# Turning three heads' normed outputs through memory with the DMA crossbar instead of on TensorE

## The chip, the cores and the metric

The kernel runs on one core of one Trainium2 chip. The metric is the device time of one execution in microseconds (us). The core has a matrix engine (TensorE, PE in the profile, with PEld for its weight loads), VectorE (DVE), ScalarE (ACT), GpSimd (POOL) and SyncE (SP), and 16 DMA engines. SyncE, ScalarE and GpSimd can issue DMAs. Each engine works through its own instructions in order.

## The reference, cut to what matters

The program is a two-layer generator trunk over 256 latent and 256 context tokens, 512 rows in all. Layer 0 uses an mLSTM mixer with four heads, layer 1 latent attention, and each is followed by a gated ConvFFN. The change sits in the mixer of layer 0, at its end:

```python
def out(h_in, s):
    Bq, T, _ = h_in.shape
    o = jax.nn.sigmoid(h_in @ w_og).reshape(Bq, T, M_HEADS, M_DV)
    hsum = o * s.transpose(0, 2, 1, 3).astype(h_in.dtype)
    return _head_rms_norm(hsum, norm_g) @ w_out
```

Each head has 512 columns (M_DV). Its gated output is divided by its root mean square over these columns, scaled with norm_g column by column, and the four heads side by side (2048 columns) are multiplied by w_out. Everything is in float32.

## The kernel before

Float32 products are made of three passes in a reduced-precision float32 (F32R): each operand is held as a high and a low part, and mm3 (line 427) issues high x high (L430), high x low (L433) and low x high (L434). The instructions are written in program order and a planner orders them on each engine: it takes, of what it expects to be ready, what comes first in the program. Tiles of one tag share a fixed number of buffers ("s2" has 15 buffers of 128x512 float32, "u" has 31 of 128x1024, "w" three), and an instruction that needs a buffer waits until one of its tag is free.

The weights come in one fixed order (class Stream): SyncE loads a block of 128x1024 (L308) into "raw", ScalarE casts it into the high part (L345), VectorE subtracts for the low part (L368), and TensorE reads both.

Background work is written as generators in k.bg. tick() advances the first generator in the list by one step after each chunk of the foreground product, so a generator starts only when the ones before it have ended; drain() runs all to the end.

The order in build() around the change:

- For each head h of four, w_qk (L999) makes its queries and keys: eight chunks of 24 matmuls of 512 columns, two ticks after each. Beside it run post(h-2), which norms and turns the output of the head two before, and head(h-1) (L1041), which makes that head's attention-like matrix and transposes it on TensorE into "PT" (L1118). Late in it v_load (L1128) loads v and the gate o ("oh") from memory into s2 buffers.
- av (L1163) multiplies PT with v, and VectorE multiplies the gate into the result (L1178): four tiles tt of 128 rows x 512 columns, in the buffers of "oh". s_mm makes the scores of the next head.
- After the last head the output product begins. outmm (L1524) runs over k = 0 to 15 (128 columns of the 2048 each, four per head) into "y" for the 256 context rows; a step k is twelve matmuls of 512 columns. k = 0 to 7 (heads 0 and 1) run with head(3) and post(2) beside them, and v_steps loads v and the gate of head 3. Then av(3); then k = 8 to 11 (head 2) with post(3) beside; then k = 12 to 15 (head 3). After that the same sixteen k for the 256 latent rows, from the same hn.

post (L1183) takes the four tiles tt of one head. ScalarE squares them and sums the rows (L1188), one Sqrt, VectorE the reciprocal (L1190) and the product with it (L1192). Then for each of four column groups e, TensorE transposes the four 128x128 blocks (L1198) into one PSUM tile "hnT", ScalarE writes it times norm_g as the high part (L1205) and VectorE the low part (L1206) of hn[k], k = 4h + e. hn[k] holds 128 columns on the partitions and all 512 rows along the free axis.

Of the kernel before, what the change touches and what calls it, by code (L numbers as in the profile page):

```python
# [7 lines left out]
F32 = mybir.dt.float32  # L8
F32R = mybir.dt.float32r
I32 = mybir.dt.int32  # L10
AF = mybir.ActivationFunctionType
ALU = mybir.AluOpType
AX = mybir.AxisListType
# [20 lines left out]
NB, NRAW, NU, NS = 3, 3, 31, 15  # L34
# [366 lines left out]
class K:  # L401
# [41 lines left out]
    def split(self, hi, lo, src):  # L443
        self.nc.scalar.copy(hi, src)
        self.nc.vector.tensor_sub(lo, src, hi)

    def smc(self, name):
        o, n = self.off[name]
        return self.sm0[:, o:o + n] if o < NSM0 else self.sm[:, o - NSM0:o - NSM0 + n]
# [25 lines left out]
    def setup(self):  # L475
# [3 lines left out]
        self.sm0 = p.tile([128, NSM0], F32, name="sm0")  # L479
        jp = p.tile([128, 128], I32, tag="s2", name="jp", bufs=NS)  # L480
        nc.gpsimd.iota(jp, pattern=[[1, 128]], base=0, channel_multiplier=-1)
# [88 lines left out]
    def ada_all(self, items):  # L570
# [14 lines left out]
        for r in self.bc:  # L585
            nc.scalar.activation(r, r, AF.Silu)  # L586
        yield
# [5 lines left out]
    def mod_tile(self, k):  # L593
# [3 lines left out]
        for g in range(2):  # L597
# [4 lines left out]
            else:  # L602
                nc.scalar.activation(v, v, AF.Identity, bias=sh[:, k, c:c + 1], scale=sc[:, k, c:c + 1])

    def start_up(self):
# [41 lines left out]

        self.tc.keep_in_program_order(nc.scalar.activation(self.tiny(1, "pre"), self.keps, AF.Silu))
        e = mybir.EngineType
# [3 lines left out]
        with self.tc.manual_schedule(engines={e.PE, e.DVE, e.Activation}):  # L653
            for _ in range(WARM):
                nc.tensor.matmul(idle, self.zero[:, 0:128], self.zero, start=True, stop=True)
            for step in STEPS:
                op, n = step[0], [int(x) for x in step[1:]]
                g = n[0]
                if op == "Q":
                    nc.scalar.activation(self.cond[:, :, 0:2], self.smc("cond").rearrange("p (a b) -> p a b", b=2),  # L660
                                         AF.Silu)
                    nc.vector.tensor_scalar(self.ident, self.jp, 0.0, None, op0=ALU.is_equal)
# [24 lines left out]
                elif op == "e":  # L687
# [3 lines left out]
                    nc.vector.tensor_scalar(x[:, c], x[:, c], sc[:, 1:2], sh[:, 1:2], op0=ALU.mult, op1=ALU.add)  # L691
                    nc.scalar.activation(h[:, 0, l], x[:, l], AF.Identity, bias=sh[:, 0:1], scale=sc[:, 0:1])
                    nc.vector.tensor_copy(h[:, 0, c], x[:, c])
# [31 lines left out]
    def conv(self, ps, w3, b, tmp, n):  # L725
        nc = self.nc
        nseg = n // 256
        nc.scalar.activation(tmp[:, :n], ps[:, :n], AF.Identity, bias=b, scale=w3[1])
        t3 = tmp[:, :n].rearrange("p (s t) -> p s t", s=nseg)
# [450 lines left out]
        self.PT = self.vh = self.oh = None  # L1180
        return r

    def post(self, h, tt):  # L1183
        nc = self.nc
        ss = self.tiny(4, "ss")
        jk = self.s2("jk")
        for t in range(4):
            nc.scalar.activation(jk, tt[t], AF.Square, accum_out=ss[:, t:t + 1])  # L1188
        nc.scalar.activation(ss, ss, AF.Sqrt, bias=self.keps, scale=1.0 / 512.0)
        nc.vector.reciprocal(ss, ss)  # L1190
        for t in range(4):
            nc.vector.tensor_scalar(tt[t], tt[t], ss[:, t:t + 1], None, op0=ALU.mult)  # L1192
        yield
        g = self.smc("mng")
        for e in range(4):
            pt = self.ps("hnT")
            for t in (2, 0, 1, 3):
                q = nc.tensor.transpose(pt[:, t * 128:(t + 1) * 128], tt[t][:, e * 128:(e + 1) * 128], self.ident)  # L1198
                if e or t != 2:
                    self.behind(q, [lead])  # L1200
                else:
                    lead = q
            k = h * 4 + e
            u = self.u("hn")
            nc.scalar.activation(u[:, 0], pt, AF.Copy, scale=g[:, k:k + 1])  # L1205
            nc.vector.scalar_tensor_tensor(u[:, 1], pt, g[:, k:k + 1], u[:, 0], op0=ALU.mult, op1=ALU.subtract)  # L1206
            self.hn[k] = u
        yield


    def bcast(self, row, name):
# [123 lines left out]
    def aout_fin(self, o1, pl, xr, gate, fi, h1u, att):  # L1335
# [86 lines left out]
        def cols(t, pts, n):  # L1422
            mod(t, 0, pts)
            for k in range(0, n, 2):
                mod(t, k + 1, pts)
                split(t, k, 0)
                split(t, k + 1, 0)
                if k + 2 < n:
                    mod(t, k + 2, pts)
                split(t, k, 1)  # L1430
                split(t, k + 1, 1)
# [750 lines left out]
def build(tc, off, a, out):  # L2182
    es = ExitStack()
    with es:
        k = K(tc, es, off, a)
        nc = k.nc
# [12 lines left out]
        k.bg2.append(k.ada_all([(0, 3, 4, 8)] + [(l, c, 0, 8) for l, c in ((0, 4), (0, 5), (1, 0), (1, 1), (1, 2), (1, 3), (1, 4), (1, 5))]))  # L2199
        S = None  # L2200
        tt = None
        k.hn = {}
        for h in range(H0):
            gens = []
            if h == 0:
                gens.append(k.gate_chain())
            if h >= 2:
                gens.append(k.post(h - 2, tt))
            if h >= 1:
                gens.append(k.head(h - 1, S))  # L2210
            k.bg = gens
            k.w_qk(h, 2, (lambda: k.v_load(h - 1)) if h >= 1 else None)
            k.drain()
            if h >= 1:
                tt = k.av(h - 1)
            S = k.s_mm(h)
        k.xc = None
        hn = lambda i: (k.hn[i][:, 0], k.hn[i][:, 1])
        pc = k.acc4()
        k.bg = [k.head(3, S, True), k.post(2, tt)]  # L2220
        vs = k.v_steps(3)
        for i in range(8):
            k.outmm("mout", range(i, i + 1), hn, pc, 0, 16, 2, n2=ADA_M)
            next(vs, None)
        k.drain()
        tt = k.av(3)
        k.bg = [k.post(3, tt)]
        k.outmm("mout", range(8, 12), hn, pc, 0, 16, 1, n2=ADA_M)
        k.drain()
        tokr = a["tok"].rearrange("(t p) d -> t p d", p=128)  # L2230
# [19 lines left out]
        pl = k.acc4()  # L2250
# [70 lines left out]
        pl = k.acc4(True)  # L2321
# [18 lines left out]
        pl = k.acc4(True)  # L2340
# [22 lines left out]
```

## Time and profile before

| | us |
|---|---|
| time, median of 3 runs | 1346.94 |
| lowest and highest of them | 1346.42 and 1347.75 |
| span of the profiled execution | 1345.3 |
| TensorE busy in that span | 1334.9 |
| VectorE busy | 1059.0 |
| ScalarE busy | 711.7 |
| GpSimd busy | 141.5 |

The times are of whole executions; the span is from the first to the last instruction of one profiled execution. A row of the profile names the line of the kernel, the engine, the operation, and output <- inputs by the program's names. "waits" rows say who waited for whom: total us, times, longest. A timeline row begins with its start and its length in us. An issue row gives the number of DMAs, KB each, and the median us from issue to landing.

### The profile page before, as it was taken

Reading aid. Unit: us, or ns where it says so; the run is one execution under the profiler, and the core shown is the slowest. Engines: PE = TensorE matmul, PEld = TensorE weight load, DVE = VectorE, ACT = ScalarE, POOL = GpSimd, SP = SyncE. Lnnn points to the kernel's source line nnn. Section 1 sums busy time; section 2 is a strip of 40 time slices with the busy share of each in tenths; the row PEclk is TensorE's granted clock in tenths of the full one; section 3 lists DMA queues with packets and bytes.
Section 4 is the critical chain, followed back from the end, with each engine's and each line's share of the span. In section 5 each row is a group of like instructions: output and inputs, shape, how many; then the busy total and the mean of one; then the engine's idle time right before and its main releaser. Section 6 shows DMA issues by size and latency. Waiting matters only on the chain.

```text
span 1345.3 us, 18750 instructions
## 1 busy us (share of the span) xinstructions
PE 1334.9 (99%) x6659; PEld 1120.2 (83%) x6659; DVE 1059.0 (79%) x1745; ACT 711.7 (53%) x1252; POOL 141.5 (11%) x236
## 2 busy tenths in 40 slices
PE   9999999999999999999999999999999999999997
PEld 5777888888888888888898888888888998988886
DVE  4798656678688696897979977758899889898874
ACT  4765444445744546474644334333566767676660
POOL 0222000011101011020002011111000002000100
PEclk9999999999999999999999999999999999999999
DMA  9988848889686384776628989967866437376750
GB/s 364 330 277 279 281 163 248 233 272 307 235 281 230 102 255 149 228 292 222 215 86 261 328 260 286 282 181 184 300 223 194 157 104 219 127 212 189 263 189 32
DMA packets 99885, 304.02 MB, mean 226 GB/s; under 512 B 12312, under 2 KB 25112, under 8 KB 99712
## 3 DMA queue, kind: packets, MB, share of 16 engines
q1 hardware_dynamic: 62992, 218.65, 48.6%
q0 software_dynamic: 26000, 66.75, 17.9%
q10 hardware_dynamic: 10800, 17.44, 3.6%
q8 instruction: 52, 0.85, 0.3%
q14 instruction: 41, 0.34, 0.1%
HBM read 272.21 MB, written 42.12 MB: 234 GB/s over the span
## 4 chain that ended last, share of the span: by engine, by line
PE 97%; DMA 1%; DVE 1%; ACT 0%; issue 0%; SPq 0%; DVEq 0%; ACTq 0%
PE fin L1503 8%; PE tok L430 6%; PE tok L434 6%; PE tok L433 6%; PE fin L433 6%; PE fin L434 6%; PE y L433 6%; PE fin L430 6%; PE y L434 6%; PE y L430 6%; PE qk L430 4%; PE qk L433 4%; PE qk L434 4%; PE up L718 2%; PE up L430 2%; PE up L434 1%
## 5 line engine op out<-in xcount | busy, mean ns | idle before, releaser
L368 DVE TENSOR_TENSOR w<-raw,w 128x1024 fp32r<-128x1024 f32 (+2 forms) x286 | 343.2, 1203 | 131.9 <-ACT w L345 129.7
L345 ACT CAST w<-raw 128x1024 fp32r<-128x1024 f32 (+2 forms) x286 | 296.2, 1037 | 282.4 <-PE tok L434 77.8
L544 DVE SCALAR_TENSOR_TENSOR junk<-ar,bc 128x1024 f32<-128x1024 f32 x128 | 156.1, 1219 | 5.2 <-ACT bc L586 2.3
L433 PE MATMUL fin<-h,w 128*128 128x512 f32 (+1 forms) x370 | 139.6, 377 | 0.0
L430 PE MATMUL fin<-h,w 128*128 128x512 f32 (+1 forms) x370 | 139.5, 377 | 0.0
L434 PE MATMUL fin<-h,w 128*128 128x512 f32 (+1 forms) x370 | 139.3, 377 | 0.0
L1503 PE MATMUL fin<-h,w 128*128 128x512 f32 (+1 forms) x636 | 111.1, 337 | 0.0
L1503 PEld LDWEIGHTS fin<-h,w 128*128 128x128 f32 x636 | 97.6, 190 | 13.2
L430 PE MATMUL qk<-xc,w 128*128 128x512 f32 x256 | 100.2, 391 | 0.0
L434 PE MATMUL qk<-xc,w 128*128 128x512 f32 x256 | 99.8, 390 | 0.0
L433 PE MATMUL qk<-xc,w 128*128 128x512 f32 x256 | 99.6, 389 | 0.0
L433 PEld LDWEIGHTS fin<-h,w 128*128 128x128 f32 x370 | 69.6, 188 | 13.0
L430 PEld LDWEIGHTS fin<-h,w 128*128 128x128 f32 x370 | 69.6, 188 | 12.9
L434 PEld LDWEIGHTS fin<-h,w 128*128 128x128 f32 x370 | 69.6, 188 | 12.6
L434 PEld LDWEIGHTS qk<-xc,w 128*128 128x128 f32 x256 | 48.0, 188 | 10.1
L430 PEld LDWEIGHTS qk<-xc,w 128*128 128x128 f32 x256 | 48.1, 188 | 9.8
L433 PEld LDWEIGHTS qk<-xc,w 128*128 128x128 f32 x256 | 48.1, 188 | 9.8
L430 PE MATMUL tok<-w,hT 128*128 128x512 f32 x128 | 49.9, 390 | 0.0
L433 PE MATMUL tok<-w,hT 128*128 128x512 f32 x128 | 49.8, 389 | 0.0
L434 PE MATMUL tok<-w,hT 128*128 128x512 f32 x128 | 49.8, 389 | 0.0
L735 ACT ACTIVATE fg<-fg 128x512 f32<-128x512 f32 (+1 forms) x44 | 23.1, 525 | 50.0 <-DVE fg L733 43.9
L368 DVE TENSOR_TENSOR wu<-raw,wu 128x1024 fp32r<-128x1024 f32 (+1 forms) x37 | 43.8, 1203 | 3.5 <-ACT wu L345 3.2
(486 smaller groups left out, 3125.7 us busy)
## 6 DMA issues: line engine op xcount, KB each, us to landing
raw<-in_ws SPq DMA_DIRECT2D x282, 512.0 KB, 4.5
ar<-in_adaT SPq DMA_DIRECT2D x80, 512.0 KB, 6.0
t4d<-in_ws POOLq DMA_DIRECT2D x20, 512.0 KB, 9.1
adaw<-in_ada SPq DMA_DIRECT2D x16, 512.0 KB, 8.0
zr<-fd ACTq DMA_DIRECT2D x33, 128.0 KB, 4.6
xmd<-xr POOLq DMA_DIRECT2D x16, 256.0 KB, 4.4
xcd<-cv POOLq DMA_DIRECT2D x16, 256.0 KB, 4.9
xs<-xmd POOLq DMA_DIRECT2D x16, 256.0 KB, 6.0
```

The lines of the kernel that those rows point to most:

```text
L345: self.cast = k.nc.scalar.copy(h[:, :cols], src)
L368: i = self.k.nc.vector.tensor_sub(l[:, :n], src, h[:, :n])
L430: q = mm(out, w[0], x[0], start=start, stop=False, skip_group_check=on)
L433: mm(out, w[0], x[1], start=False, stop=False, skip_group_check=on)
L434: mm(out, w[1], x[0], start=False, stop=stop, skip_group_check=on)
L544: nc.vector.scalar_tensor_tensor(o, w, 1.0, self.bc[j], op0=ALU.mult, op1=ALU.mult, accum_out=col[:, k, j:j + 1])
L718: nc.tensor.matmul(ps[m], wk[i][:, c], hT[k][:, j], start=made[m] == 0, stop=made[m] == 23)
L735: nc.scalar.activation(tmp[:, :n], tmp[:, :n], AF.Silu)
L1503: self.nc.tensor.matmul(ps[:, 0:256] if x else ps, w[x][:, k * 128:(k + 1) * 128], h[:, 0:256] if x else h, start=i == 0 and not k0, stop= ...
```

## The change

For heads 0, 1 and 2, post ends after the norm. ScalarE writes each normed tile as two planes of 16-bit halves (first the even half words of a row, then the odd ones), GpSimd writes the planes to memory, and the head and its place in memory are put in a list. A new generator turn_heads, placed behind head() in k.bg, takes it from there: SyncE issues four crossbar-transposing DMAs, one for each column group, each reading 1024 rows of 128 half words (two per token, one of each plane) and leaving 128 partitions of 1024 half words, which are the 512 float32 words in their order. From these SBUF tiles "hx" ScalarE and VectorE make the high and low part of hn as before. Head 3 (last=True) is turned on TensorE as before.

```diff
+U16 = mybir.dt.uint16
...
+    def planes(self, dst, src):
+
+        i = self.nc.scalar.copy(dst, src.bitcast(U16).rearrange("p (n h) -> p h n", h=2))
+        return i
...
-    def post(self, h, tt):
+    def post(self, h, tt, last=False):
...
         for t in range(4):
             nc.vector.tensor_scalar(tt[t], tt[t], ss[:, t:t + 1], None, op0=ALU.mult)
         yield
+        if not last:
+            d = self.dr.tile([512, 2, 512], U16, name="hd")
+            for t in range(4):
+                pl = self.pool.tile([128, 2, 512], U16, tag="s2", name="pl", bufs=NS)
+                self.planes(pl, tt[t])
+                nc.gpsimd.dma_start(d[t * 128:(t + 1) * 128], pl)
+            self.turned.append((h, d))
+            yield
+            return
         g = self.smc("mng")
...
+    def turn_heads(self):
+
+        nc, g = self.nc, self.smc("mng")
+        h, d = self.turned.pop(0)
+        v = d.rearrange("t h n -> (t h) n")
+        xs = []
+        for e in range(4):
+            x = self.s2("hx")
+            nc.sync.dma_start_transpose(x.bitcast(U16), v[:, e * 128:(e + 1) * 128])
+            xs.append(x)
+            if e % 2:
+                yield
+        for e in range(4):
+            k, x = h * 4 + e, xs[e]
+            u = self.u("hn")
+            nc.scalar.activation(u[:, 0], x, AF.Copy, scale=g[:, k:k + 1])
+            nc.vector.scalar_tensor_tensor(u[:, 1], x, g[:, k:k + 1], u[:, 0], op0=ALU.mult, op1=ALU.subtract)
+            self.hn[k] = u
+            xs[e] = x = None
+            if e % 2:
+                yield
...
-        k.hn = {}
+        k.hn, k.turned = {}, []
...
             if h >= 1:
                 gens.append(k.head(h - 1, S))
+            if h >= 2:
+                gens.append(k.turn_heads())
...
-        k.bg = [k.head(3, S, True), k.post(2, tt)]
+        k.bg = [k.head(3, S, True), k.post(2, tt), k.turn_heads()]
...
-        k.bg = [k.post(3, tt)]
+        k.bg = [k.post(3, tt, True)]
```

## The prediction

> **What bounds the kernel now.** I read the span and clock of the core first, then the page's busy shares and the chain that ended last, then all waits of TensorE.
>
> ```profile
> core 0: 1345.3 us, clock 0.998
> PE 1334.9 (99%) x6659; PEld 1120.2 (83%) x6659; DVE 1059.0 (79%) x1745; ACT 711.7 (53%) x1252; POOL 141.5 (11%) x236
> PE 97%; DMA 1%; DVE 1%; ACT 0%; issue 0%; SPq 0%; DVEq 0%; ACTq 0%
> PE idle L655 <- DVE adav L497: 1.5, 1, 1.5
> PE adar L509 <- DMA adaw<-in_ada: 0.5, 1, 0.5
> PE up L718 <- DVE hT L693: 0.3, 1, 0.3
> PE y L433 <- DVE w L368: 0.2, 1, 0.2
> ```
>
> TensorE is 97% of the chain and waits 2.5 us in all, most of that in the start-up. So work taken off TensorE is worth its whole length, and a wait put in front of TensorE costs its whole length. ScalarE (53%) and the DMA queues matter only where they make TensorE late. What the removed transposes cost is read from the chain in order of time (start, length, what), since a matmul's own duration overlaps the next one:
>
> ```profile
> 465.16 1.94 PE hnT L1198 x16
> 524.35 1.94 PE hnT L1198 x16
> 598.62 1.75 PE hnT L1198 x16
> 615.38 1.75 PE hnT L1198 x16
> ```
>
> These are heads 0, 1, 2 and 3. The change takes away the first three groups: 1.94 + 1.94 + 1.75 = **5.63 us** of the chain, 0.42% of the span.
>
> **The change part by part.** *Heads 0 and 1* are turned while w_qk of heads 2 and 3 runs, and their first reader is the output product, "y". By the order of the ticks the crossbar DMAs come after head() of the next head, which ends with the transposes "PT":
>
> ```profile
> 487.55 1.31 PE PT L1118 x12
> 546.74 1.31 PE PT L1118 x12
> 576.57 0.39 PE L430 MATMUL y<-w,hn 128*128 128x512 f32 x1
> 467.33 0.23 PE qk L433
> 455.00:514.00 59.00, 59.00 (x281) 49.17 (x280) 47.19 (x96) 30.09 (x65) 6.42 (x12) 1.00 0.61 189
> 467.18 1.65 POOL L1133 DMA_DIRECT2D vr<-vd  x3 [43.37 <-PE hnT L1198]
> 494.85 2.18 ACT L444 CAST v<-vr 128x512 fp32r<-128x512 f32 x4
> 554.78 2.49 DVE L445 TENSOR_TENSOR v<-vr,v 128x512 fp32r<-128x512 f32 x4
> 564.23 0.39 PE L430 MATMUL av<-v,PT 128*128 128x512 f32 x1
> ```
>
> So about 490 us for head 0, read from 576.57 on, and about 549 us for head 1, read four steps of k later (2.72 us each, below), at 587.5: 38 us and more of reserve, and the path through memory is covered by the qk products. What could leak is a delay of something else. The window row is the stretch of one head (busy time of PE, PEld, DVE, ACT, POOL, then clock 1.00, DMA share 0.61 and GB/s): ScalarE works 30 of 59 us, so four more copies fit. The loads of v wait for buffers of the tag s2 that the old transposes freed; now the half-word planes and the turned tiles take eight more of the 15. But v is loaded at 467 and cast only at 494.85, 26 us of reserve, and split 7.0 us before "av" reads it (554.78 + 2.49 against 564.23). On SyncE a crossbar DMA waits for the four writes, with weight loads behind it; on ScalarE the copy into hn waits for the crossbar, with the next weight cast behind it. One qk chunk is 24 matmuls of 0.23 us, 5.5 us, and the three weight buffers hold two chunks ahead, some 11 us less the 2.2 us of cast and subtraction (L345 and L368 below). Against a landing of 4 to 8 us I cost heads 0 and 1 at nothing; without that cover each us of lateness would be a us of TensorE.
>
> *The added work* in rows. The plane copy writes 128x1024 half words; the trace has no such copy, the nearest is the weight cast of 128x1024 (mean ns after the bar's first number):
>
> ```profile
> L368 DVE TENSOR_TENSOR w<-raw,w 128x1024 fp32r<-128x1024 f32 (+2 forms) x286 | 343.2, 1203 | 131.9 <-ACT w L345 129.7
> L345 ACT CAST w<-raw 128x1024 fp32r<-128x1024 f32 (+2 forms) x286 | 296.2, 1037 | 282.4 <-PE tok L434 77.8
> L1205 ACT ACTIVATE hn<-hnT,sm x16: 674/684/700, 466.0 to 618.1; 128x512 fp32r<-128x512 f32 x16
> L1206 DVE SCALAR_TENSOR_TENSOR hn<-hnT,sm,hn x16: 741/743/751, 467.3 to 619.6; 128x512 fp32r<-128x512 f32 x16
> ```
>
> So 4 x 1.04 = 4.2 us of ScalarE a head, 12.5 us in all (elements of half the width may go faster or, with a stride, slower; I take the row, half and double would be 2.1 and 8.3 a head). The copy and subtraction into hn stay (0.68 and 0.74 us), only their source moves from PSUM to SBUF.
>
> *Head 2* is where it is decided. Its post() runs beside the output product of rows k = 0 to 7, and k = 8 to 11 read its hn right after "av" of head 3. The timelines of TensorE, VectorE, ScalarE, SyncE and GpSimd there:
>
> ```profile
> 609.77 0.39 PE L430 MATMUL y<-w,hn 128*128 128x512 f32 x1
> 612.49 0.39 PE L430 MATMUL y<-w,hn 128*128 128x512 f32 x1
> 597.38 1.26 DVE L1192 TENSOR_SCALAR oh<-oh,ss 128x512 f32<-128x512 f32 x3
> 596.43 1.15 ACT L444 CAST v<-vr 128x512 fp32r<-128x512 f32 x2
> 604.13 0.33 SPq L308 DMA_DIRECT2D raw<-in_ws  x1
> 615.04 1.75 SPq L308 DMA_DIRECT2D raw<-in_ws  x4
> 592.60 2.12 POOL L1566 DMA_DIRECT2D xres<-in_tok  x4
> DMA  0588899999997892000028999479500797999940
> ```
>
> The first row is k = 8, the second the next k: 2.72 us a step. Head 3's "av" stays, so with 1.75 us of transposes gone TensorE reaches k = 8 at 609.77 - 1.75 = **608.0** on the trace's clock (the earlier 3.88 us shift both sides alike). Ready is: VectorE ends the norm at 598.6 and ScalarE its v casts at 597.6; four plane copies from there, 597.6 + 4.2 = 601.8 (the last tile's norm is in time); GpSimd issues a write in a quarter of 2.12 us, 0.53: 602.3. Landing and turning, by the issue rows (KB each, median us to landing; the last one from the window 590 to 640):
>
> ```profile
> x3d<-z POOLq DMA_DIRECT2D x4, 256.0 KB, 2.3
> xmd<-xr POOLq DMA_DIRECT2D x16, 256.0 KB, 4.4
> raw<-in_ws SPq DMA_DIRECT2D x6, 256.0 KB, 4.2
> out_dram<-z SPq DMA_DIRECT2D x2, 256.0 KB, 2.0
> t4d<-in_ws POOLq DMA_DIRECT2D x4, 256.0 KB, 11.4
> xres<-in_tok POOLq DMA_DIRECT2D x8, 256.0 KB, 7.8
> ```
>
> A write of 256 KB by GpSimd: from 2.3 to 7.8 us (the busy shares of the DMA engines, 1.25 us a digit from 590, are 7 to 9 until 608.75, when these writes go); I take 4.4, the like write of 256 KB: 606.7. The crossbar pass is in no row: from 2.0 (any 256 KB on SyncE) to 11.4 (the slowest 256 KB); I take 4.2, the 256 KB load on SyncE: 610.9. Copy and subtraction, 0.68 + 0.74 = 1.4: hn of k = 8 is there at **612.3**, TensorE stands 612.3 - 608.0 = **4.3 us**. The three other passes I take as overlapped, since the four xres loads issued within 2.12 us all land in about 7.8; then they come closer than the 2.72 us a step and add nothing. With the ends: 602.3 + 2.3 + 2.0 + 1.4 = 608.0, no wait, and 602.3 + 7.8 + 11.4 + 1.4 = 622.9, 14.9 us. Plane copies of half and double length move these by -2.1 and +4.2, and GpSimd may hold the writes behind an xres load that waits for a buffer.
>
> TensorE has nothing else to do in that wait: k = 9 to 11 need the same head, the weights come in one order. Behind the waiting crossbar on SyncE stand the four loads of 615.04, which wait for the same steps anyway; behind the waiting copy on ScalarE the cast for k = 11 and the squares of head 3, whose reader is k = 12, three steps later; behind the writes on GpSimd xres and gate, read after k = 15. Those I cost at nothing.
>
> **Sum:** -5.63 + 4.3 = -1.3 us: span 1345.3 - 1.3 = 1344.0. The median of the runs, 1346.94, stands 1.6 us above the span of the profiled execution, so the forecast is **1345.6 us**, 0.1% below: no change that a measurement of this kernel can tell (about 0.2%, 2.7 us).
>
> [...]
>
> **The rivals.** *Hidden (0.32):* write and pass together take under 7.2 us (8.6 above), or the planner's order gives the chain a lead, so that TensorE waits under 2.9 us. For it: the DMA engines are empty from 608.75 on, so a pass has them alone. Against it: the writes go while they are full. Time with no wait: 1346.94 - 5.63 = 1341.3.
>
> *Slower (0.21): the passes come one by one.* If each crossbar pass waits for the one before it, pass n lands at 606.7 + 4.2n, the fourth at 623.5, with hn at 624.9; k = 11 is due at 608.0 + 3 x 2.72 = 616.2. That is 8.7 us of wait, and 12.1 with a write of 7.8. Net +3.1 to +6.5: 1350.0 to 1353.4, say **1352**. It decides from 4.1 us a pass on, where the wait passes 8.3 us (5.63 + 2.7). Against it: plain loads on one queue overlap, as above.
>
> *Much slower (0.06):* passes one by one, at the slowest row: 606.7 + 4 x 11.4 + 1.4 - 616.2 = 37.5 us of wait, 1378.8. [...]
>
> *Not what it says (0.05):* the time taken off TensorE does not come back even for heads 0 and 1, since a late copy into hn holds back a weight cast or v on ScalarE. It decides when the copy waits more than the 7.0 us reserve of v; at 3 us a head beyond it, 1345.6 + 6 = 1351.6.
>
> **How the numbers follow.** Forecast 0.36, with its own range 1344.2 to 1349.6 (a wait of 2.9 to 8.3 us). Faster by over 0.2% is the hidden case: 0.32. Within 0.2% is the forecast: 0.36. Slower is the three others: 0.32. The range goes from 1340.8 (no wait, and half a us of disorder in its favour) to 1355 (a late write, serial passes, some us of disorder); outside lie the much slower case and the tails, under 0.2.
>
> **What would show it.** Transposes "hnT" down from 64 to 16. A wait of TensorE before "y" of k = 8, released by VectorE's subtraction into hn, of about 4 us; none in the w_qk stretches, which end 1.9 us earlier each. Writes of the planes landing in 4 to 5 us and the passes in about as much, overlapped. The forecast is wrong if no such wait is there (the chain had more lead than I gave it), if four passes lie one behind the other, or if waits appear before "av" or "qk".

## The result, and the profile after

The changed kernel takes **1371.7 us** (median of four runs, 1368.3 to 1372.21) against 1346.93 us for the kernel before on the same chip: a ratio of 1.018, with a 95% interval of 1.0166 to 1.0193. It is slower by some 24.8 us, where the prediction had 1345.6 us and a range of 1340.8 to 1355.0. In the changed file the lines of mm3 are L431, L434 and L435, "PT" is L1124, the planes L450, their writes L1205, the crossbar passes L1233, and the copy and subtraction into hn L1240 and L1241.

Span and clock of the core after the change, then from its page the busy times of the engines and their shares of the chain of work that ended last:

```profile
core 0: 1369.8 us, clock 0.989
PE 1337.6 (98%) x6611; PEld 1120.0 (82%) x6611; DVE 1059.0 (77%) x1745; ACT 723.6 (53%) x1264; POOL 147.9 (11%) x248
PE 84%; issue 9%; DVE 3%; DMA 3%; ACT 1%; POOL 1%; SPq 0%; DVEq 0%; POOLq 0%; ACTq 0%
```

The largest new waits of TensorE after the change (who waited for whom: total us, times, longest):

```profile
PE y L431 <- ACT hn L1240: 13.6, 2, 12.6
PE PT L1124 <- DVE W L1111: 7.4, 2, 4.2
...
PE hnT L1213 <- DVE oh L1198: 1.0, 1, 1.0
```

The span grew by 24.5 us. TensorE does 48 transposes less (x6659 before, x6611 now), the 5.63 us of the prediction, and yet it is busy 2.7 us longer (1337.6 against 1334.9). So three terms make the difference: 5.63 us gained; 21.8 us of new idle time (1369.8 - 1337.6 = 32.2 against 1345.3 - 1334.9 = 10.4), which is the rows of "y", "PT" and "hnT" above, 22.0 us; and 5.63 + 2.7 = 8.3 us in which the same matmuls took longer. -5.63 + 21.8 + 8.3 = 24.5.

The 12.6 us before "y" are head 2, the wait that was forecast at 4.3. The waits of "PT" for W were not forecast: they are in the queries and keys of heads 2 and 3, where the cost was put at nothing. The windows show the third term (busy time of PE, PEld, DVE, ACT and POOL, then the granted clock, DMA share and GB/s), and the chain in order of time shows what it is:

```profile
455.00:520.00 65.00, 60.84 (x272) 50.52 (x271) 42.01 (x87) 34.10 (x69) 8.54 (x16) 0.95 0.80 187
...
585.00:630.00 45.00, 32.36 (x147) 26.45 (x146) 26.05 (x65) 22.96 (x47) 10.73 (x20) 0.90 0.79 222
```

```profile
469.66 7.93 DMA aB<-ad
...
492.41 1.97 PE PT L1124 x8
494.38 0.42 PE qk L431
...
498.13 0.23 PE qk L431
```

The kernel before has a clock of 1.00 in both; its row of the second (the prediction shows one of 455 to 514):

```profile
585.00:630.00 45.00, 45.00 (x222) 37.68 (x221) 37.37 (x68) 26.15 (x51) 8.62 (x16) 1.00 0.59 210
```

After a pause, here the 4.2 us before "PT" at 492.41, a matmul takes 0.42 us in place of 0.23 until 498 (granted clock 0.50 from 492 to 496 and 0.53 from 496 to 498), and only then the old 0.23 (1.00 from 498 to 500). The three pauses of over 3 us (12.6, 4.2 and 3.2) so cost some 8 us more than they last.

The first row of that chain tells where the late W came from: a load "aB" of 7.93 us, issued at 469.66. GpSimd's timeline says why it is issued then, after the change (its last row is for head 2, below) and, in the second fence, before:

```profile
466.29 0.54 POOL L1205 DMA_DIRECT2D hd<-pl  x1 [55.13 <-ACT pl L450]
...
467.77 0.55 POOL L1051 DMA_DIRECT2D aB<-ad  x1
...
469.66 0.54 POOL L1051 DMA_DIRECT2D aB<-ad  x1
...
611.34 2.21 POOL L1603 DMA_DIRECT2D xres<-in_tok  x4
```

```profile
418.19 0.54 POOL L1045 DMA_DIRECT2D aB<-ad  x1 [7.19 <-DVE junk L544]
```

aB is the first thing that head() needs for W, two loads for each head. Before, GpSimd issued them at 418.19 and 422.28, and their first reader started at 454.83. Now the first write of the planes stands ahead of them in GpSimd's order, GpSimd sits idle for 55.13 us until a plane copy is there, and the loads are held back with it: they go out at 467.77 and 469.66, nearly 50 us later.

For head 2 the rows are SyncE's four passes (the start of the first, then how long SyncE was held by all four) of each head, and ScalarE's first copy into hn:

```profile
480.53 19.62 SPq L1233 DMA_TRANSPOSE hx<-hd  x4
540.63 8.80 SPq L1233 DMA_TRANSPOSE hx<-hd  x4
613.93 20.57 SPq L1233 DMA_TRANSPOSE hx<-hd  x4
```

```profile
628.33 0.72 ACT L1240 ACTIVATE hn<-hx,sm 128x512 fp32r<-128x512 f32 x1 [16.96 <-DMA hx<-hd]
```

Four passes held SyncE for 8.8 us in one place and about 20 in the two others. Beside the last four, GpSimd loads the residual rows "xres" (from 611.34); before the change those loads went at 592.60 (quoted in the prediction), ahead of this place. The first pass is issued at 613.93 and the first copy into hn starts at 628.33, 14.4 us later.

### The profile page after: what moved, and what is told of

It reads as the page before. It is cut to its first block, busy times and chain, and to the rows that moved or that the text cites. A ratio compares the mean times of both kernels' runs of the same rounds, so it can differ in the third digit from the quotient of the medians.

```text
span 1369.8 us, 18713 instructions
## 1 busy us (share of the span) xinstructions
PE 1337.6 (98%) x6611; PEld 1120.0 (82%) x6611; DVE 1059.0 (77%) x1745; ACT 723.6 (53%) x1264; POOL 147.9 (11%) x248
## 4 chain that ended last, share of the span: by engine, by line
PE 84%; issue 9%; DVE 3%; DMA 3%; ACT 1%; POOL 1%; SPq 0%; DVEq 0%; POOLq 0%; ACTq 0%
PE fin L1540 8%; PE tok L431 6%; PE tok L435 6%; PE tok L434 6%; PE fin L434 6%; PE fin L435 6%; PE fin L431 6%; PE y L434 5%; PE y L431 5%; PE y L435 5%; PE up L724 2%; PE up L431 1%; PE up L434 1%; PE up L435 1%; PE qk L431 1%
## 5 line engine op out<-in xcount | busy, mean ns | idle before, releaser
L434 PE MATMUL fin<-h,w 128*128 128x512 f32 (+1 forms) x370 | 139.6, 377 | 0.0
L431 PE MATMUL fin<-h,w 128*128 128x512 f32 (+1 forms) x370 | 139.5, 377 | 0.0
L435 PE MATMUL fin<-h,w 128*128 128x512 f32 (+1 forms) x370 | 139.4, 377 | 0.0
L431 PE MATMUL qk<-xc,w 128*128 128x512 f32 x256 | 101.5, 397 | 0.0
L434 PE MATMUL qk<-xc,w 128*128 128x512 f32 x256 | 100.8, 394 | 0.0
L435 PE MATMUL qk<-xc,w 128*128 128x512 f32 x256 | 100.7, 393 | 0.0
L431 PEld LDWEIGHTS fin<-h,w 128*128 128x128 f32 x370 | 69.6, 188 | 12.9
L434 PEld LDWEIGHTS fin<-h,w 128*128 128x128 f32 x370 | 69.6, 188 | 12.8
L435 PEld LDWEIGHTS fin<-h,w 128*128 128x128 f32 x370 | 69.6, 188 | 12.7
L435 PEld LDWEIGHTS qk<-xc,w 128*128 128x128 f32 x256 | 48.8, 190 | 10.3
L431 PEld LDWEIGHTS qk<-xc,w 128*128 128x128 f32 x256 | 48.9, 191 | 10.1
L434 PEld LDWEIGHTS qk<-xc,w 128*128 128x128 f32 x256 | 48.8, 191 | 10.0
L431 PE MATMUL y<-w,hn 128*128 128x512 f32 x92 | 36.9, 406 | 13.6 <-ACT hn L1240 13.6
L431 PE MATMUL tok<-w,hT 128*128 128x512 f32 x128 | 49.9, 390 | 0.0
L434 PE MATMUL tok<-w,hT 128*128 128x512 f32 x128 | 49.9, 389 | 0.0
L435 PE MATMUL tok<-w,hT 128*128 128x512 f32 x128 | 49.8, 389 | 0.0
```

What stands on the lines that cost most here:

```text
L431: q = mm(out, w[0], x[0], start=start, stop=False, skip_group_check=on)
L434: mm(out, w[0], x[1], start=False, stop=False, skip_group_check=on)
L435: mm(out, w[1], x[0], start=False, stop=stop, skip_group_check=on)
```

## The experiments

**Theory A**: two independent losses. Heads 0 and 1 lose because the aB loads of head() stand behind the plane writes in GpSimd's order. Head 2 loses because its four passes take some 15 to 20 us where 4.2 us, overlapped, were forecast. **Rivals**: for heads 0 and 1, that planes and turned tiles hold the s2 buffers, so that aB waits for a buffer wherever the writes stand (B), or that the passes hold up SyncE's weight loads; for head 2, that the writing and copying is slow, not the crossbar. Later, for head 2, **A1** (the passes are slow because GpSimd's loads move beside them) against **A2** (they are slow by themselves). First came the parts, one at a time, beside 1347.13 us for the kernel before on that chip (1347.18 for the later ones, from the writes on ScalarE's queue to the first of the versions to beat both).

**Heads 0 and 1 alone.** Head 2 is turned on TensorE again:

```diff
-        k.bg = [k.head(3, S, True), k.post(2, tt), k.turn_heads()]
+        k.bg = [k.head(3, S, True), k.post(2, tt, True)]
```

> Only heads 0 and 1 go through memory, head 2 is turned on TensorE. Theory A (two separate losses: heads 0 and 1 lose 12.2 us because head()'s loads aB stand behind the half-word writes in GpSimd's queue, so the transposes PT of TensorE come late; head 2 loses 17.9 us because TensorE waits for its hn): the first stays, the second goes: about 1355, TensorE waiting some 7 us before PT and under 1 us before y. Rival B (the crossbar's stream slows every other transfer and all losses come from that): the same sign, but the size follows the passes, two thirds of them left: about 1363. Rival C (the losses feed each other, the late start of head 3's chain makes head 2 late): under 1350 and over 1345.

1354.88 us, ratio 1.0057 (1.0042 to 1.0072). The largest wait of TensorE:

```profile
PE PT L1124 <- DVE W L1111: 7.4, 2, 4.6
```

The "y" wait is gone and the "PT" wait is the same 7.4 us. As forecast.

**Head 2 alone.** Heads 0 and 1 on TensorE:

```diff
-                gens.append(k.post(h - 2, tt))
+                gens.append(k.post(h - 2, tt, True))
...
-            if h >= 2:
-                gens.append(k.turn_heads())
```

> Only head 2 goes through memory, heads 0 and 1 are turned on TensorE. Theory A: its loss stays whole, 17.9 us less the 1.75 us saved: about 1363, no wait before PT, 13 to 15 us before y of k = 8. Rival B: one third of the loss, about 1355. Rival C: smaller than A, since head 3's chain starts in time.

1362.75 us, ratio 1.0124 (1.0107 to 1.0141). TensorE's largest wait, and SyncE's row of the passes:

```profile
PE y L431 <- ACT hn L1240: 12.7, 1, 12.7
```

```profile
605.88 15.53 SPq L1233 DMA_TRANSPOSE hx<-hd  x4
```

As forecast, with the wait a little under the 13 to 15 us expected. The two parts lose 7.8 and 15.6 us, 23.4 of the 24.8: they are nearly independent.

**head() ahead of post().** In the loop the order of the generators is turned, so that aB is issued before the plane writes:

```diff
-            if h >= 2:
-                gens.append(k.post(h - 2, tt))
             if h >= 1:
                 gens.append(k.head(h - 1, S))
             if h >= 2:
+                gens.append(k.post(h - 2, tt))
                 gens.append(k.turn_heads())
```

> All three heads through memory, but in the loop of w_qk the generator head() stands before post(), so GpSimd issues the loads aB before the half-word writes. Theory A: the waits before PT go and 12.2 us come back: about 1359.5, the wait of y for head 2 stays. Rival B: aB lands late anyway under the crossbar's traffic: 1368 to 1372, waits before PT stay.

1372.83 us, ratio 1.0186 (1.0165 to 1.0208), 13 us above what theory A expected. GpSimd's row of aB, the two largest waits of TensorE, and the chain about 560:

```profile
418.43 1.06 POOL L1051 DMA_DIRECT2D aB<-ad  x2 [7.07 <-DVE junk L550]
```

```profile
PE y L431 <- ACT hn L1240: 15.9, 1, 15.9
PE PT L1124 <- DVE W L1111: 5.9, 1, 5.9
```

```profile
551.06 9.84 DMA hx<-hd
...
560.92 0.73 ACT hn L1240
...
562.93 8.30 DMA raw<-in_ws
...
571.56 0.68 DVE oh L1184
```

aB is back at 418.43 and the two "PT" waits in the weights' products are gone: the first product of the output stage starts at 576.70 us, where the changed kernel has 584.93. So the order in GpSimd's queue was the cause there. But the passes are later now: ScalarE waits 9.84 us for a turned tile, the next weights stand behind the passes in SyncE's queue and land 8.30 us after, and what follows (the gate, the scores, head 3's "PT", 5.9 us) is late in its turn.

**Plain loads in place of the passes.** The plane copy becomes a plain copy and each pass a load of the same 256 KB, so nothing is turned:

```diff
...
-        v = d.rearrange("t h n -> (t h) n")
+        v = d.rearrange("t h n -> t (h n)")
...
-            nc.sync.dma_start_transpose(x.bitcast(U16), v[:, e * 128:(e + 1) * 128])
+            nc.sync.dma_start(x.bitcast(U16), v[e * 128:(e + 1) * 128])
```

> The crossbar passes are replaced by plain loads of 256 KB of the same memory on the same queue, and the plane copy keeps the half words in their order, so hn holds rows that are not turned: the output is not the reference's. Writes, waits, copies and buffers stay. Theory A: heads 0 and 1 lose as before (aB behind the writes), head 2 waits only some 4 to 6 us: 1355 to 1359. Rival B (the crossbar itself is the whole loss): 1341 to 1346, no waits before PT. If a round trip through memory is as slow as the crossbar: 1368 to 1372.

1360.62 us, ratio 1.0104 (1.0081 to 1.0127), a little above what was expected. TensorE's waits of "PT", and of "y" for hn:

```profile
PE PT L1124 <- DVE W L1111: 7.3, 2, 4.3
...
PE y L431 <- ACT hn L1240: 0.4, 1, 0.4
```

Writing, loading and copying alone make next to no wait before "y" for hn (0.4 us); the crossbar does. The comparison isn't quite clean: a plain load reads the rows of one write only, so the first one goes out at 609.97 us, 4 us ahead of the first pass of the changed kernel. But the first copy into hn starts at 614.56 us in place of 628.33, so most of the 13.8 us are the pass. "PT" waits as long as before, without any pass: not the passes hold heads 0 and 1 up.

**The writes on ScalarE's queue.** One word of the changed kernel:

```diff
-                nc.gpsimd.dma_start(d[t * 128:(t + 1) * 128], pl)
+                nc.scalar.dma_start(d[t * 128:(t + 1) * 128], pl)
```

> The changed kernel, but its twelve plane writes are issued on ScalarE's queue, not on GpSimd's, so no aB load of head() stands behind a write that waits for its plane copy. Theory A (heads 0 and 1 lose about 8 us because the aB loads stand behind the writes in GpSimd's order; head 2 loses about 18 us to the passes): the waits of PT for W inside the weights' products shrink from 7.4 us to under 2.5, the first product of the output stage starts at 577 to 579 us instead of 584.9, the wait of y for hn stays at 11 to 14 us, and the time is 1361 to 1365. Rival B (the plane copies hold s2 buffers, and aB waits for a buffer whatever queue the writes stand in): the wait of PT stays at 7 us, the first product stays at 584 to 586, the time at 1368 to 1372.

1353.12 us, ratio 1.0044 (1.0029 to 1.0059), 8 us better than theory A expected, with a wait of "y" of 7.2 us where it had 11 to 14. The waits, and SyncE's row for head 2:

```profile
PE y L431 <- ACT hn L1240: 7.2, 1, 7.2
...
PE PT L1124 <- DVE W L1111: 1.0, 1, 1.0
```

```profile
606.66 6.16 SPq L1233 DMA_TRANSPOSE hx<-hd  x4
```

The first product of the output stage starts at 572.90 us, 3.67 before the kernel before: heads 0 and 1 give nearly all of their 3.88 us. B falls as the cause, since planes and tiles need as many buffers as in the changed kernel. Something of it is there: aB now does wait for a buffer, and is issued at 438.78 us, 20 us later than before, but that is still in time. The surprise is head 2: with the writes out of GpSimd's queue its xres loads are partly over when the passes start (six of the eight are issued by 603.6 us, the first pass at 606.66), and the four hold SyncE for 6.16 us, not 20.57. That speaks for A1.

**GpSimd's loads held back.** Head 2 alone, as above, but xres and gate are loaded only when hn of k = 11 is written, through a one-element copy of ScalarE into each buffer (the new argument "after"):

```diff
...
-        xr = k.res_load(tokr, 0)
-        gate = k.bcast(k.gd[0, 2][1:2, :], "gate")
+        turned = k.hn[11][0:1, 0, 0:1].bitcast(F32)
+        xr = k.res_load(tokr, 0, after=turned)
+        gate = k.bcast(k.gd[0, 2][1:2, :], "gate", turned)
...
```

> Heads 0 and 1 on TensorE, head 2 through memory, and the loads of the residual rows and of the gate, which GpSimd issues in the output stage, held back until the last turned block of head 2 is written (a one-element copy on ScalarE ahead of each). Theory A1 (the passes of head 2 are slow because those loads move at the same time): the four passes on SyncE's queue take under 10 us together instead of 15.5, the wait of y for hn falls from 12.7 us to 4 to 6, and the time is 1351 to 1356, unless the late residual rows become a wait of their own. Theory A2 (the passes are slow by themselves, or through the weight loads of SyncE): the passes stay at 13 to 16 us, the wait at 11 to 14, the time at 1361 to 1365.

1350.12 us, ratio 1.0023 (1.0014 to 1.0032), 12.6 us better than with the loads beside the passes, and a little better than A1 expected. The wait, the chain, and the passes on SyncE's queue (ns min, median and max, first and last start):

```profile
PE y L431 <- ACT hn L1240: 2.9, 1, 2.9
```

```profile
605.39 4.76 DMA hx<-hd
...
610.17 0.73 ACT hn L1240
```

```profile
L1233 SPq DMA_TRANSPOSE hx<-hd x4: 1237/1250/2170, 605.4 to 610.4; - x4
```

The same pass in head 2 alone is on its chain too:

```profile
605.88 14.41 DMA hx<-hd
...
620.32 0.73 ACT hn L1240
```

4.76 us against 14.41 from the issue of the first pass to the copy that reads it, with nothing changed but GpSimd's loads: A1.

**The price of a pass by itself.** Kernel before, with four passes of 256 KB more behind the last output product of the mixer, once with little beside them (weight loads, and one load of 256 KB that GpSimd issues at 668.46), and once with four more GpSimd loads of 256 KB started at the same time (the first loop, in the second kernel only):

```diff
...
+        for s in range(4):
+            nc.gpsimd.dma_start(ys[s], k.vd[1, s])
+        for e in range(4):
+            nc.sync.dma_start_transpose(xs[e].bitcast(mybir.dt.uint16), vu[:, e * 128:(e + 1) * 128])
```

> The kernel before, with four crossbar passes of 256 KB more, of the first 512 rows of the stored v, issued on SyncE one after the other behind the last output product of the mixer, into buffers that nothing reads; it measures the price of a pass with few other transfers beside it. Theory A1: a pass lands in 2 to 3 us after the one before (the four in 8 to 12 us), and SyncE is held for most of that. Theory A2: 5 us each, about 20 us, as in the changed kernel's slow groups. The time isn't the point; it may rise by a few us where SyncE's later loads stand behind the passes.

> The kernel before with the four crossbar passes behind the mixer's last output product, as in the run with the passes alone (1.3 us for the first on SyncE, 8.4 us for the other three, with weight loads of SyncE beside them), and four loads of 256 KB on GpSimd at the same time. Theory A1 (GpSimd's transfers and the passes hold each other up): the four take 14 to 20 us on SyncE and the four loads land in 8 to 15 us. Theory A2: about 10 us as without them, the loads in 4 to 6 us.

One execution each; the views of the tile "xb" (the passes: ns min, median and max on SyncE's queue) and, in the second kernel, also of the GpSimd loads "yb" with their us to landing:

```profile
L2262 SPq DMA_TRANSPOSE xb<-vd x4: 1263/1806/4572, 668.1 to 676.6; - x4
```

```profile
L2267 SPq DMA_TRANSPOSE xb<-vd x4: 1251/2340/8773, 670.1 to 684.4; - x4
...
L2265 POOL DMA_DIRECT2D yb<-vd x4: 536/536/538, 670.0 to 671.6; - x4
DMA to landing us min/median/max: 6.1/10.3/13.1
```

Both came out as A1 said. The first pass holds SyncE for 1.26 us in either kernel. The four together hold it for 9.6 us with little beside them and for 14.9 us beside the four loads (4.6 and 8.8 us for the longest), and a pass lands in 7.5 and 10.5 us (median). The loads land in 10.3 us (median), where other GpSimd loads of 256 KB in the same execution, "xres", have medians of 3.5 to 7.8; so the loads seem to pay too, but no run has these loads without the passes.

**Versions to beat both.** The first: heads 0 and 1 only, head() ahead of post(), and the split into hn as a generator of its own that runs later (its body is left out here).

```diff
...
-            if h >= 2:
-                gens.append(k.post(h - 2, tt))
             if h >= 1:
                 gens.append(k.head(h - 1, S))
             if h >= 2:
+                gens.append(k.post(h - 2, tt))
                 gens.append(k.turn_heads())
+            if h >= 3:
+                gens.append(k.split_heads(0))
...
-        k.bg = [k.head(3, S, True), k.post(2, tt), k.turn_heads()]
+        k.bg = [k.split_heads(1), k.head(3, S, True), k.post(2, tt, True)]
```

> A try for a version ahead of both: only heads 0 and 1 go through memory; head() is ahead of post() in the background of each step, so that the aB loads come before the plane writes; the passes go out one at a time into f32 buffers of their own, and the split into hn (ScalarE's copy and VectorE's subtract) is a generator of its own, one step of the loop later. Heads 2 and 3 are turned on TensorE as before. Theory A (what was lost with heads 0 and 1 was lost to the order of GpSimd's queue and to ScalarE's waiting for a pass): no wait of PT for W over 2.5 us and none of y for hn; 1.94 + 1.94 us of transposes are gone, and the time is 1342.5 to 1344.5. Rival B (a pass holds SyncE, so the next weights of qk or the raw loads come late, whatever the order): waits of 3 us and more inside the weights' products, and the time is 1347 to 1356.

1355.1 us, ratio 1.0065 (1.0053 to 1.0078). The output stage starts at 572.93, as early as theory A wants, but then:

```profile
PE PT L1124 <- DVE W L1111: 5.6, 1, 5.6
```

The time is that of rival B, and the profile shows its mechanism at work. The passes of head 1, which head() now precedes, hold SyncE from 549.56 until about 562.9 us, and the eight weight loads behind them go out 6.7 us later than before the change:

```profile
556.77 6.10 SPq L1233 DMA_TRANSPOSE hx<-hd  x2
...
562.96 13.06 SPq L309 DMA_DIRECT2D raw<-in_ws  x8
```

```profile
556.26 14.57 SPq L308 DMA_DIRECT2D raw<-in_ws  x8
```

The chain behind the wait leads back to one of these loads (8.79 us, from 564.54). TensorE doesn't wait for the weights themselves: VectorE, which makes their low parts, comes late to head(3)'s W. head() ahead of post() has the same late loads (562.93) and the same wait (5.9 us) without the new generator. In the output stage the split of head 1 also runs on VectorE ahead of head(3); what that adds was not tried by itself. The second version keeps the changed kernel's order and moves only the writes to ScalarE's queue, for heads 0 and 1; the third does so for all three heads and also holds back GpSimd's loads:

```diff
-                nc.gpsimd.dma_start(d[t * 128:(t + 1) * 128], pl)
+                nc.scalar.dma_start(d[t * 128:(t + 1) * 128], pl)
...
-        k.bg = [k.head(3, S, True), k.post(2, tt), k.turn_heads()]
+        k.bg = [k.head(3, S, True), k.post(2, tt, True)]
```

> Heads 0 and 1 through memory with their plane writes issued on ScalarE's queue, head 2 turned on TensorE as before. Theory A (what heads 0 and 1 lost was the aB loads behind the writes in GpSimd's order): no wait of PT inside the weights' products over 2 us and no wait of y for hn; the first product of the output stage at about 572.9 us, 3.7 us earlier than before, and nothing lost behind it: 1342.5 to 1344.5. Rival B (head 3's weights come late in the output stage whenever the transposes are gone, since TensorE gets there sooner, as with the first try): a wait of PT of 3 to 6 us about 590 us, and 1348 to 1355.

> All three heads through memory with the plane writes issued on ScalarE's queue, and GpSimd's loads of residual rows and gate held back until head 2 is turned. Both mended losses together: the first product of the output stage at about 572.9 us; four passes of head 2 in about 6 us, a wait of y for hn of 2 to 4 us, and some 1.5 to 2 us lost to a lowered clock behind it: 1345.5 to 1348.5, no faster than before. Rival: the passes of head 2 aren't eased further (they already took 6.16 us with ScalarE's writes), the wait stays at 7 us and the time at 1352 to 1354.

**1344.42 us** and **1344.47 us** (11 runs each) against 1347.30 (21 runs): ratios 0.998 (0.9971 to 0.9989) and 0.9982 (0.9973 to 0.9991). The second came out as theory A expected, the third 1 us below its range. Both are ahead of the kernel before by 0.2%, and of the changed one by 2%. What is left of these waits in the second version, then in the third:

```profile
PE PT L1124 <- DVE W L1111: 0.3, 1, 0.3
```

```profile
PE y L431 <- ACT hn L1240: 1.6, 1, 1.6
...
PE PT L1124 <- DVE W L1111: 1.3, 1, 1.3
```

With two heads the span falls by 3.2 us (1342.1) of 3.88 to be had. The third head takes 1.75 us more off TensorE and gives it back in waits of 1.6 and 1.3 us, so it adds nothing that can be measured.

## Why the prediction was wrong

- **The 5.63 us** hold as far as they were tried: with two heads and no waits, 3.2 of 3.88 us come back in the span.
- **"I cost heads 0 and 1 at nothing" is the first step that failed.** The prediction tested v, the weight casts and the s2 buffers, and asked for head 2 alone what stands behind the writes on GpSimd. For heads 0 and 1 it followed the writes' data (38 us of reserve, which was right) but not the queue they were put in: the aB loads of the next head stood behind them. That cost 7.4 us of waits, 7.8 us of time together with what the lowered clock took and less the transposes. With the writes in another queue most of the 3.88 us are there.
- **The crossbar pass, "I take 4.2", overlapped, is the second: right for a pass with room, wrong for this place.** Held apart from GpSimd's loads, the first pass took 4.76 us to its reader. What failed is "the DMA engines are empty from 608.75 on, so a pass has them alone", and with it the xres and gate loads behind the writes "at nothing": those were among the loads that had filled the engines up to 608.75 (DMA share 0.85 from 590 on, then 0.05 until 615), and the writes ahead of them pushed them into the empty stretch, which in the prediction's own row of digits ends at about 615 us anyway. As a reader of data they had reserve; as a neighbour of the passes they had none. The first pass took 14.4 us.
- **The terms of the added work** were right: plane copies of 1.04 us were forecast, the weight cast's row; they measured 1.037 to 1.059 us. The writes landed in 4.0 us (4.4 taken; the median of twelve). One small step was wrong: TensorE waits for ScalarE's copy into hn alone, not for VectorE's subtraction (0.74 us). With the loads held back the first pass also goes out 2.8 us after the last write was issued (602.57 to 605.39) and not 4.4, and so the wait was 2.9 us where 4.3 were forecast.
- **The lowered clock was in no step.** Of the 24.5 us, 8.3 are matmuls at a lower clock behind the waits. The prediction said that a wait "costs its whole length"; it costs more.
- **The rivals.** In number "much slower" (1378.8) came nearest, and that is luck: it had 37.5 us of wait at head 2, where 12.6 were, and nothing at heads 0 and 1. "Not what it says" had the loss at heads 0 and 1, but by late copies on ScalarE. "Slower: the passes come one by one" had the place of the larger loss; but crowded passes, not serial ones, were the mechanism: in the kernel with the loads held back SyncE is done with a pass in 1.25 us (median), while the first took 4.76 us to its reader, so they overlap. With room four passes begin at 605.39 there and the DMA engines have gone quiet by about 613 (the rows are in the last section); the first is 4.76 us from its reader, and behind the mixer a pass lands in 7.5 us, against the 4.2 of a plain load that the forecast took. Beside GpSimd's loads the first is 14.4 us from its reader.

## What to carry to other kernels

When work moves to a DMA, ask of the queue that issues it what stands behind a transfer that waits for its data: loads that had been there some 25 us before they were read became the bound, because one waiting write put ahead of them moved them by nearly 50. An empty stretch of the DMA engines is empty only in the old order; look which transfers the change pushes into it. And price a wait of TensorE like these at its length and some 2 to 3 us besides (1.8 to 3.5 here, for waits of 2.9 to 12.7 us, each alone in its kernel).

## What was not expected of the hardware

The granted clock after a pause of TensorE, in windows of head 2 alone (a pause of 12.7 us up to 621) and of the kernel with the loads held back (2.9 us up to 611):

```profile
621.00:627.00 6.00, 5.91 (x14) 4.65 (x15) 3.01 (x4) 3.60 (x9) 1.07 (x2) 0.51 0.61 155
627.00:633.00 6.00, 6.00 (x28) 4.93 (x28) 4.31 (x6) 4.09 (x9) 0.00 (x0) 1.00 0.29 87
```

```profile
611.00:613.00 2.00, 2.00 (x8) 1.59 (x9) 1.43 (x2) 1.38 (x4) 0.00 (x0) 0.84 1.04 201
613.00:615.00 2.00, 2.00 (x6) 1.59 (x5) 1.02 (x2) 1.70 (x4) 0.00 (x0) 0.50 0.06 13
615.00:617.00 2.00, 2.00 (x8) 1.61 (x7) 1.11 (x2) 1.71 (x10) 0.28 (x1) 0.81 0.00 0
```

Half the clock for nearly six us after the long pause, and for about three and a half after the short one, there beginning only when TensorE was already at work again. After the pause of 1.6 us in the third version the clock stayed at 1.00. The full clock was back some 5.8 us after TensorE went to work again behind the long pause and some 4.8 us behind the short one, and a pause of 2.9 us was enough here. What the runs lost to it, as the busy time of TensorE above what its fewer transposes leave (the kernel before and the two with four passes more, with the same work and no such pause, differ by up to 1.3 us, so small values mean little):

| kernel | pauses of 2 us and more, us | TensorE busy | more than its work, us |
|---|---|---|---|
| changed | 12.6, 4.2, 3.2 | 1337.6 | 8.3 |
| plain loads | 4.3, 3.0, 2.1 | 1337.6 | 8.3 |
| head() ahead of post() | 15.9, 5.9 | 1335.6 | 6.3 |
| heads 0 and 1 alone | 4.6, 2.8 | 1335.1 | 4.1 |
| first version to beat both | 5.6, 2.4 | 1335.7 | 4.7 |
| writes on ScalarE's queue | 7.2 | 1332.8 | 3.5 |
| head 2 alone | 12.7 | 1336.1 | 3.0 |
| head 2 alone, loads held back | 2.9 | 1334.9 | 1.8 |
| three heads, both mended | none (1.6 the longest) | 1330.5 | 1.2 |
| two heads, writes on ScalarE's queue | none | 1331.3 | 0.3 |

The loss goes by the number of pauses rather than by their length: 12.7 us in one piece cost 3.0, and the plain loads lose as much as the changed kernel with half its waits. The other surprise is that a crossbar pass beside GpSimd's loads is so much slower: three times in head 2 alone (14.41 against 4.76 us to the reader), by half for the four passes behind the mixer (14.9 against 9.6 us on SyncE). What they share was not tried out; the runs show only that it goes away when they are apart in time.
